# Small unused loads of a few rows each, put on three engines' queues between the large transfers of a cross-covariance attention kernel

## The chip, the cores and the metric

One core of one Trainium2 chip runs the kernel. The time is the device time of one execution in microseconds (us). The core has five engines that work side by side (PE multiplies matrices, DVE, ACT and POOL work on vectors, SP only issues transfers) and 16 DMA engines that move data between HBM and the on-chip memory. An engine runs its own instructions in order; engines wait for one another, and for transfers, through semaphores.

## The reference

Q, K and V are 8 x 12 x 512 x 64 in float32, as is the output: 12.58 MB each, 37.75 MB read and 12.58 MB written.

```
Q_norm = Q / (norm(Q, axis=-2) + 1e-10)          # over the 512 rows of a head
K_norm = K / (norm(K, axis=-2) + 1e-10)
attn   = softmax(einsum('bhnd,bhne->bhde', Q_norm, K_norm), axis=-1)   # 64 x 64 per head
out    = einsum('bhnd,bhde->bhne', V, attn)
```

## The kernel before

**Tiles.** The 96 heads are taken in S = 12 steps of 8 heads. A step loads one Q tile and one K tile (`load_qk`, L211-221, 128 partitions x 2 x 4 KB, 1 MB each), casts them to bfloat16 (`cast_qk`), squares them for the norms (`square`), forms the grams on PE (`grams`, L260), and goes through norms, softmax and scaling to `ab`. V comes in 12 tiles of 1 MB (`load_v`, L223-225, rows of 8 KB), is cast (`cast_v`), transposed on PE and multiplied with `ab` (`outs`, L338); `ocopy` brings the result to `so`, and `store` (L227-234) writes 1 MB per step. Step 0 loads its Q and K as halves of 512 KB, K's two from ACT's queue, all else from SP's. In all there are 52 transfers, 50 issued by SP and 2 by ACT.

**The cut store.** The store of step S - 3 (`PAR['SPLIT']`, `PAR['CUTS']`, L229-232) is written as three: 68 rows, 60 rows, and 128 rows of 4 KB.

**Order.** `Order` (L70 on) is a list scheduler that runs while the program is built: every piece of work is added with its cost, what it comes after and a rank; `plan.run()` fixes the order, and the loop at L484 emits the pieces in it. The order of the instructions on each engine is then fixed.

**Completion semaphores.** A transfer issued by SP or ACT takes, in the order of the program, the next of eight completion semaphores in turn (they are called slots below), and the built program makes its issue wait until the transfer eight places before it, which held the same slot, has landed. A semaphore counts to 16 for one transfer. As SP issues in order, all that stands behind a waiting issue waits too. At most eight of these transfers are thus in flight.

**Buffers.** Q and K share seven buffers (`NB['qk']`), V has three, `so` has six; a load also waits until the casts that read its buffer before are done.

Of the kernel before, what the change touches and what calls it, by code (L numbers as in the profile page):

```python
# [8 lines left out]
F32 = mybir.dt.float32  # L9
# [140 lines left out]
def kernel(  # L150
# [7 lines left out]
    nc = tc.nc  # L158
# [190 lines left out]
    def parts(s):  # L349
        return (0, 1) if s in FINE else (None,)  # L350

    for c in parts(0):
# [4 lines left out]
        name=nc.get_next_instruction_name(), engine=mybir.EngineType.Activation, ins=[], outs=[], act_func_set_id=LN_EXP))  # L357
# [29 lines left out]
    def v_at(v):  # L387
        return PAR["V_FROM"] + PAR["V_PACE"] * (v / W)
# [3 lines left out]
    def piece(key, engines, after, behind, rank, fn, *args):  # L392
        if key[0] in CHOICE:
            engines = {e: (c, BIAS.get((key[0], e), 0.0)) for e, c in engines.items()}
            plan.add(key, engines, after, behind, rank, lambda eng: fn(eng, *args))
        else:
            plan.add(key, engines, after, behind, rank, lambda eng: fn(*args))
# [46 lines left out]
    for w in range(W):  # L444
        for r in range(2):
            n = 2 * w + r - NB["v"]
# [22 lines left out]
    for s in range(S):  # L469
        for x in range(4):  # L470
            n = 4 * s + x - 2
# [7 lines left out]
        for i in halves(s):  # L479
            order = [("st", s, 0) if i else ("st", s - 1, halves(s - 1)[-1]) if s else None]  # L480
            piece(("st", s, i), {"DMA": 2 * X if i is None else X}, [("oc", s, x) for x in range(4)], order, v_at(0.5 * s) + PAR["ST_LAG"], store, s, i)

    ahead = [(k, 0, c) for c in parts(0) for k in ("lq", "lk")]
    for (emit, eng), (_, _, key, _) in zip(plan.run(), plan.order):  # L484
        if key not in ahead:
            emit(eng)


# [28 lines left out]
```

## Time and profile before

| | us |
|---|---|
| median of 2 runs (128.31 to 128.37) | 128.34 |
| the profiled execution, its own time | 128.12 |
| its span on the core | 126.0 |
| busy: PE 81.7, ACT 85.0, DVE 79.4, POOL 46.5 | |
| last instruction that computes ends | 114.8 |
| last store lands | 124.9 |

The page of the profile gives busy times by engine, a timeline in 40 slices, the DMA queues, and the chain of work that ended last. The timeline has lines for the DMA engines' busy share and for the GB/s moved. Queue q1 is that of SP's transfers, q10 that of ACT's, q8 fetches instructions. Beside the page, the trace keeps each DMA packet with its start, duration and size, and each count of a completion semaphore with its time; these are called packet records and counts below.

### The profile page before, as it was taken

To read this page: it belongs to the slowest core of one execution; us is meant where nothing else is said; L and a number is where in the kernel's file an instruction comes from. 1 tells how busy PE (TensorE), PEld (TensorE's weight loads), DVE (VectorE), ACT (ScalarE), POOL (GpSimd) and SP (SyncE) were. 2 spreads that over 40 slices of the span, in tenths; PEclk is the share of its full clock that TensorE was granted. 3 is DMA by queue.
4 is the path that set the end of the run, shared out by engine and by line. 5 is a ranking of instruction groups with operands and counts; after the bars stand their busy time and mean duration, and the time that the engine had idled before them with its cause. 6 is when DMAs were issued, how large, how long until landed. Compare 5 with 4: busy or idle time off the path is not lost.

```text
span 126.0 us, 4061 instructions
## 1 busy us (share of the span) xinstructions
PE 81.7 (65%) x1800; PEld 54.2 (43%) x1800; DVE 79.4 (63%) x140; ACT 85.0 (67%) x116; POOL 46.5 (37%) x40
## 2 busy tenths in 40 slices
PE   0009459894598787869578898864799878951000
PEld 0006145571474465557335556451387446630000
DVE  2223343899853989988987599993789998700000
ACT  4086668595697854998799987929839885864000
POOL 3250665470637098062707916144324700000000
PEclk9999999999657999995959999998559999996555
DMA  3999999999999999999999999999999999999982
GB/s 107 416 420 428 432 411 423 421 419 414 430 415 428 416 427 412 419 414 427 414 436 415 416 419 412 442 399 421 433 416 416 411 420 411 419 412 423 406 359 85
DMA packets 11588, 50.59 MB, mean 402 GB/s; under 512 B 819, under 2 KB 819, under 8 KB 10035
## 3 DMA queue, kind: packets, MB, share of 16 engines
q1 hardware_dynamic: 11283, 49.29, 95.3%
q10 hardware_dynamic: 288, 1.05, 2.0%
q8 instruction: 14, 0.23, 0.6%
q14 instruction: 3, 0.02, 0.0%
HBM read 37.75 MB, written 12.58 MB: 399 GB/s over the span
## 4 chain that ended last, share of the span: by engine, by line
DMA 54%; PE 15%; DVE 11%; ACT 6%; SPq 3%; issue 2%; ACTq 0%
DMA qk<-in_Q_dram 31%; DMA v<-in_V_dram 17%; DMA qk<-in_K_dram 6%; PE po L338 4%; ACT so L205 3%; PE l L266 3%; PE gram L260 3%; SPq L225 3%; DVE ab L310 2%; PE vps L323 2%; PE gram L289 2%; DVE s L271 1%; ACT sq L251 1%; DVE vt L207 1%; ACT vb L205 1%
## 5 line engine op out<-in xcount | busy, mean ns | idle before, releaser
L209 POOL TENSOR_SCALAR kb<-qk 128x2048 bf16<-128x2048 f32 (+1 forms) x13 | 23.4, 1802 | 38.1 <-DMA qk<-in_K_dram 35.0
L205 ACT COPY so<-po 128x512 f32<-128x512 f32 x47 | 25.6, 583 | 4.0 <-PE po L338 2.9
L251 ACT ACTIVATE sq<-qb 128x2048 bf16<-128x2048 bf16 (+1 forms) x13 | 23.1, 1778 | 7.7 <-DVE qb L207 7.6
L209 POOL TENSOR_SCALAR vb<-v 128x1024 bf16<-128x1024 f32 x15 | 20.1, 1355 | 13.7 <-DMA v<-in_V_dram 13.7
L338 PE MATMUL po<-ab,vt 128*32 128x128 bf16 x768 | 21.0, 237 | 6.0 <-ACT ex L299 1.6
L260 PE MATMUL gram<-qb,kb 32*128 32x128 bf16 x768 | 15.6, 240 | 12.2 <-POOL kb L209 9.6
L266 PE MATMUL l<-sq,hm 128*32 128x512 bf16 x96 | 19.5, 470 | 1.7 <-ACT sq L251 1.1
L323 PE MATMUL vps<-ident,vb 128*128 128x128 f32 x96 | 17.2, 305 | 4.4 <-POOL vb L209 2.3
L207 DVE CAST qb<-qk 128x2048 bf16<-128x2048 f32 (+1 forms) x12 | 13.6, 1135 | 10.0 <-DMA qk<-in_Q_dram 9.9
L260 PEld LDWEIGHTS <-kb 32*128 32x128 bf16 x768 | 13.4, 106 | 14.3 <-POOL kb L209 10.9
L338 PEld LDWEIGHTS <-vt 128*32 128x32 bf16 x768 | 14.3, 103 | 12.0 <-issue 7.7
L207 DVE COPY vt<-vps 128x1024 bf16<-128x1024 bf16 (+1 forms) x25 | 16.5, 664 | 3.0 <-PE vps L323 2.8
L251 ACT ACTIVATE sq<-kb 128x2048 bf16<-128x2048 bf16 (+1 forms) x10 | 17.3, 1734 | 0.7 <-POOL kb L209 0.7
L205 ACT CAST vb<-v 128x1024 bf16<-128x1024 f32 x9 | 12.1, 1344 | 6.8 <-DMA v<-in_V_dram 6.6
L323 PEld LDWEIGHTS vps<-ident,vb 128*128 128x128 f32 x96 | 11.3, 152 | 8.2 <-POOL vb L209 3.1
L271 DVE TENSOR_REDUCE s<-l 64x128 f32<-64x512 f32 x12 | 8.1, 678 | 8.5 <-PE l L266 8.5
L289 PE MATMUL gram<-ident,kqs 128*128 128x128 f32 x48 | 9.7, 336 | 3.5 <-DVE kqs L285 3.1
L295 DVE TENSOR_TENSOR ls<-gram,r 64x256 f32<-64x256 f32 x24 | 10.1, 420 | 2.7 <-PE gram L289 2.5
L285 DVE TENSOR_TENSOR kqs<-gram,r 128x512 f32<-128x512 f32 x12 | 8.2, 687 | 3.2 <-ACT r L281 2.6
L266 PEld LDWEIGHTS <-hm 128*32 128x32 bf16 x96 | 5.7, 108 | 9.7 <-issue 7.8
L310 DVE TENSOR_TENSOR ab<-ex,rb 128x512 bf16<-128x512 f32 x12 | 9.4, 781 | 0.4
L289 PEld LDWEIGHTS gram<-ident,kqs 128*128 128x128 f32 x48 | 6.2, 166 | 7.5 <-DVE kqs L285 6.6
(25 smaller groups left out, 41.3 us busy)
## 6 DMA issues: line engine op xcount, KB each, us to landing
v<-in_V_dram SPq DMA_DIRECT2D x12, 1024.0 KB, 19.5
qk<-in_Q_dram SPq DMA_DIRECT2D x11, 1024.0 KB, 19.6
qk<-in_K_dram SPq DMA_DIRECT2D x11, 1024.0 KB, 19.7
out_dram<-so SPq DMA_DIRECT2D x11, 1024.0 KB, 17.4
qk<-in_K_dram ACTq DMA_DIRECT2D x2, 512.0 KB, 6.0
qk<-in_Q_dram SPq DMA_DIRECT2D x2, 512.0 KB, 5.7
out_dram<-so SPq DMA_DIRECT2D x1, 512.0 KB, 10.0
out_dram<-so SPq DMA_DIRECT2D x1, 272.0 KB
```

The lines of the kernel that those rows point to most:

```text
L205: nc.scalar.copy(o, i)
L207: nc.vector.tensor_copy(o, i)
L209: nc.gpsimd.tensor_scalar(out=o, in0=i, scalar1=1.0, scalar2=0.0, op0=ALU.mult, op1=ALU.add)
L251: nc.scalar.activation(o, i, AF.Square)
L260: nc.tensor.matmul(gram[s][:, h, 0], k, q, start=(t == 0), stop=(t == TT - 1))
L266: nc.tensor.matmul(st[s][32 * x:32 * (x + 1)].rearrange("p t d -> p (t d)"), hm, sq[s][:, x, t:t + 4].rearrange("p t r d -> p (t r d)"), s ...
L271: nc.vector.tensor_reduce(out=s2[s], in_=st[s].rearrange("p t d -> p d t"), axis=mybir.AxisListType.X, op=ALU.add)
L289: nc.tensor.transpose(gram[s][:, h, 1], kqs[s][:, h], ident)
L295: nc.vector.tensor_tensor(out=ls[s][half], in0=gram[s][half, :, 1, half], in1=r12[s][half, :HU, None].to_broadcast([D, HU, D]), op=ALU.mult)
L310: nc.vector.tensor_tensor(out=ab[s], in0=ex[s][:, :, None, :].to_broadcast([128, HU, 2, D]), in1=rb[:, :, :, None].to_broadcast([128, HU, ...
L323: nc.tensor.transpose(ps[:, n], vb[w][:, j].rearrange("p r d c -> p (r d c)").bitcast(F32), ident)
L338: nc.tensor.matmul(po[s, x][32 * h:32 * (h + 1), j].rearrange("p r d -> p (r d)"), v, ab[s][:, h].rearrange("p r d -> p (r d)"), start=Tru ...
```

## The change

A function `mark` issues a load of n rows of K, of a few float32 words each, into a tile that nothing reads. After every planned transfer, from the seventh on, `marked` issues up to three of them: on SP's queue loads of 1, 2, ... 15 rows of 16 words, then one row of 18 words and 17 rows of 19 words; on ACT's queue eight loads of 1, 1, 2, 3, 5, 7, 17 and 20 rows of 20 to 34 words; on POOL's queue seven of 1, 1, 2, 3, 5, 17 and 24 rows of 42 to 54 words. The output does not depend on any of them.

```
+    marks = ctx.enter_context(tc.tile_pool(name="marks", bufs=1))
+    Km = K.rearrange("b h n d -> (b h n) d")
+    seen = [0]
+
+    shared = {q: (marks.tile([128, w], F32, name=f"marks{w}"), [0]) for q, w in ((nc.sync, 16), (nc.scalar, 36), (nc.gpsimd, 56))}
+
+    def mark(queue, n, words, at=0):
+        seen[0] += 1
+        if queue in shared and not (queue is nc.sync and words != 16):
+            m, next_row = shared[queue]
+            at = next_row[0]
+            next_row[0] += n
+        else:
+            m = marks.tile([128, words], F32, name=f"mark{seen[0]}")
+        queue.dma_start(out=m[at:at + n, 0:words], in_=Km[0:n, 0:words])
+
+    def marked(i):
+        if 1 <= i <= 15:
+            mark(nc.sync, i, 16)
+        for queue, gap, first, sizes in ((nc.scalar, 1, 3, (1, 1, 2, 3, 5, 7, 17, 20)), (nc.gpsimd, 2, 2, (1, 1, 2, 3, 5, 17, 24))):
+            k, rest = divmod(i - first, gap)
+            if rest == 0 and 0 <= k < len(sizes):
+                mark(queue, sizes[k], (20 if queue is nc.scalar else 42) + 2 * k)
+        if i == 16:
+            mark(nc.sync, 1, 18, 100)
+        if i == 17:
+            mark(nc.sync, 17, 19)
+
     ahead = [(k, 0, c) for c in parts(0) for k in ("lq", "lk")]
+    count = 0
     for (emit, eng), (_, _, key, _) in zip(plan.run(), plan.order):
         if key not in ahead:
             emit(eng)
+        if eng == "DMA":
+            count += 1
+            marked(count - 6)
```

The built program has 77 transfers on the eight slots in place of 52 (67 on SP, 10 on ACT), and 7 on POOL with semaphores of their own that only the end of the kernel waits for. The other instructions stand in the order they had. These are the first 33 of the 77, numbered in the order of the slots; a number n waits until n - 8 has landed. mS is a small load on SP with its rows, mA one on ACT; Q2 is the Q tile of step 2, V0 the first V tile.

```
 0 Q0a   1 K0a(ACT)  2 Q0b    3 K0b(ACT)  4 Q1     5 mA 1   6 K1    7 V0
 8 mA 1  9 mA 2     10 mA 3  11 mS 1     12 V1    13 mA 5  14 mA 7 15 mS 2
16 Q2   17 mA 17    18 mS 3  19 K2       20 mA 20 21 mS 4  22 V2   23 mS 5
24 Q3   25 mS 6     26 K3    27 mS 7     28 Q4    29 mS 8  30 K4   31 mS 9
32 V3
```

From 22 on, large loads and SP's small ones take turns up to number 47 (the load of 17 rows); from 48 on there are only large transfers.

## The prediction, written before the changed kernel was run

> **What bounds the kernel now.** I read the page's timeline first, then its queue table, then the busy times by stretch, then SP's own order of time.
>
> The page's timeline and queues:
>
> ```profile
> DMA  3999999999999999999999999999999999999982
> GB/s 107 416 420 428 432 411 423 421 419 414 430 415 428 416 427 412 419 414 427 414 436 415 416 419 412 442 399 421 433 416 416 411 420 411 419 412 423 406 359 85
> DMA packets 11588, 50.59 MB, mean 402 GB/s; under 512 B 819, under 2 KB 819, under 8 KB 10035
> ...
> q1 hardware_dynamic: 11283, 49.29, 95.3%
> q10 hardware_dynamic: 288, 1.05, 2.0%
> q8 instruction: 14, 0.23, 0.6%
> ```
>
> All 16 DMA engines are busy from the second slice to the last but one; no other engine is over 67%. The kernel is bound by its 50.3 MB, at about 421 GB/s, or 2.49 us for each 1 MB transfer. Busy times by stretch show the end:
>
> ```profile
> 110.00:115.00 5.00, 2.40 (x96) 1.46 (x88) 0.39 (x1) 3.51 (x7) 0.00 (x0) 0.94 1.02 413
> 115.00:120.00 5.00, 0.00 (x0) 0.00 (x0) 0.00 (x0) 0.00 (x0) 0.00 (x0) 0.50 1.02 413
> 120.00:123.00 3.00, 0.00 (x0) 0.00 (x0) 0.00 (x0) 0.00 (x0) 0.00 (x0) 0.50 0.85 350
> 123.00:126.00 3.00, 0.00 (x0) 0.00 (x0) 0.00 (x0) 0.00 (x0) 0.00 (x0) 0.50 0.18 72
> ```
>
> The five numbers before the last three are the engines' busy times, the last two the DMA share and GB/s. Computing ends at 114.8 us; the DMA engines need ten more. So computing can run some us late without moving the end, while every us that a DMA engine on the path loses is lost for good. From 120 us on the share falls: the 16 DMA engines do not end together. The counts of the last store show it: the 16 arrive from 121.06 to 124.91 us, three by 121.22, two more by 122.82, nine from 123.92 to 124.27, then 124.67 and 124.91. The span is set by the one engine that is last.
>
> SP's instructions in order of time, at the start:
>
> ```profile
> 5.42 0.38 SPq L219 DMA_DIRECT2D qk<-in_Q_dram  x1
> 5.84 0.47 SPq L219 DMA_DIRECT2D qk<-in_K_dram  x1
> 7.91 0.34 SPq L225 DMA_DIRECT2D v<-in_V_dram  x1
> 8.30 1.18 SPq L219 DMA_DIRECT2D qk<-in_Q_dram  x1
> 10.68 2.53 SPq L219 DMA_DIRECT2D qk<-in_K_dram  x1
> 13.31 3.12 SPq L219 DMA_DIRECT2D qk<-in_Q_dram  x1
> ```
>
> Start, duration, what. An issue takes 0.34 to 0.47 us; from 8 us on each lasts until there is room, since up to eight transfers are in flight (a Q load lands 19.6 us after its issue by the page, nearly 8 x 2.49). The queue is eight deep, far more than is needed to keep the engines fed.
>
> **The change part by part.** Nothing is removed. Added are 25 issues on the slots and 7 on POOL.
>
> *Issues on SP, 17.* At 0.33 us each (the cut stores' issues, the cheapest on SP, took 0.33 to 0.40) they are 5.6 us of SP, which has nothing to do but to keep the queue full. Cover: the transfers in flight. The small loads take slots, so fewer large ones are ahead. I walked through the list of slots with the landing times of before. Number 15 (mS 2) waits for 7 (V0, landed 15.5), and behind it on SP stands 16 (Q2). At that moment V1 alone is in flight, 2.49 us of work. Of it go 0.45 us (the 16 counts of one transfer are that far apart then), 0.33 us for the issue of mS 2, and about 1.0 us from the start of Q2's issue to its first packet (the first issue of the kernel: 0.74 to 1.75 us). 0.7 us are left: no gap, but a narrow place. Next K2 (19) goes out at about 16.8, V2 (22) at about 17.8; from Q3 on (waits for Q2, 20.5) three large transfers are in flight or more, 7.5 us of cover. Bounds for this place: 0 by these rows; 0.9 us lost if a small issue under load lasts as long as the median K issue, 1.93 us (1.93 - 0.33 - 0.7). I take 0, nearest to rows of like size. If the cover is gone, each us of delay is a us of time.
>
> *Issues on ACT, 8.* At 0.40 us (K's issues of before) 3.2 us, between 2.9 and 21 us, where ACT is idle 0.50, 1.23, 0.91, 0.31, 1.17 us between its instructions. Behind each stands ACT's next square or copy. Their waits are for transfers landed by then: the mA of 2 rows needs K0a (5.6) and comes after a square that ends 7.2; that of 20 rows needs V1 (18.0) and comes after one that ends at 20.2. Three gate SP in turn: mA 7 (14) gates V2, mA 17 gates mS 6, mA 20 gates Q4. mA 7 can go out when the square of Q1 ends, 13.8, and V2 has until about 22 us. ACT runs late by 1 to 2 us around 20 us; hidden by the ten us at the end. Cost 0.
>
> *Issues on POOL, 7.* The trace has no DMA issue on POOL. Between 0.33 us (SP's) and 1.9 us (POOL's longest instruction) each. POOL waits for data before the casts behind them: 3.84 (two of them), 1.31, 3.60, 1.17, 1.80, 3.91 us. At most 0.7 us late at one cast; hidden likewise. Cost 0.
>
> *Packets.* This is the cost that lands on the path. Rows: SP's 1 + ... + 15 + 1 + 17 = 138, ACT's 56, POOL's 76 (the two loads of one row go as 14 and 11 pieces), 270 small packets, and about 264 counts (4-byte packets; 122 from SP, 30 from ACT by the split below, 16 for each on POOL taken). How many DMA engines share them? The counts of before tell: the store of 68 rows got 12 of its 16 counts at its issue (109.6 us) and four at 117.10, 117.23, 117.76 and 117.82; that of 60 rows got one at once and 15 later; 128 rows all 16 late. So 4, 15 and 16 engines: the largest number up to 16 that divides the rows. A load of n rows up to 15 then lies on n engines, 17 rows on one, 20 on ten. I take the first engines to be used each time. Engine 0 then carries 15 + 1 + 17 rows from SP and 6 + 17 + 2 from ACT, 58, with some from POOL about 60, and 25 counts; engines 1 to 3 carry about 20, 18 and 16 rows and as many counts. The Trainium skill has the same in DMA: Bandwidth & Descriptors, "Why a DMA increments its semaphore by 16 and not by 1", and adds that the lowest-numbered engines are used on SP's and ACT's queues; the counts above agree with the numbers 4 and 15, and no run so far shows which engines they are. Spread evenly instead, 270 rows would be 17 an engine, and the sum below would be 0.4 us.
>
> The price of one row: the packet records have 9 ns for 4 bytes, 8 ns for 40 bytes, 156 to 159 ns for 4096 and 309 for 8192 bytes. A line through the last two is 9 ns + 0.037 ns a byte, 11 to 17 ns for 64 to 216 bytes. Ends: 9 and 159 ns. I take 20 ns, near the small rows, a little above the line since no packet of before reads so short a row from HBM. Engine 0: 60 x 20 + 25 x 9 = 1.4 us. Engines 1 to 3: 20 x 20 + 18 x 9 = 0.55 us. The same page, "Specifications", says that transfers under 512 bytes read, modify and write. That speaks for a dearer row; no record of before shows it, and it gives no figure.
>
> *What of it reaches the end.* The four engines of the 68 rows have 44 rows of 4 KB to go, 44 x 0.156 = 6.9 us: they end at 124.0, 124.1, 124.6 and 124.7. The last two counts, 124.67 and 124.91, are thus two of these four, and these four are the ones that get most of the small rows. If engine 0 is one of the late two: +1.4 us. If one of the early two (0.9 earlier): 1.4 - 0.9 = 0.5, and engines 1 to 3 give 0.55. The mean of 1.4 and 0.55 is 1.0 us.
>
> *Sum:* 128.12 + 0 + 0 + 0 + 1.0 = 129.1 for the profiled execution. The median of the runs shown is 0.22 above that execution, so 129.4.
>
> **The rivals.**
> - *Hidden.* The rows cost 9 ns, or engine 0 is an early one: 60 x 9 + 25 x 9 = 0.77, less than its 0.9 of room, and the others 0.3: about 128.5. For it: the 40-byte records. Against it: all four engines are close to the end. It needs no luck beyond a cheap row.
> - *The queue runs dry (slower).* At number 15 the wait for V0 leaves V1 alone in flight. If the small load's issue, or the wake-up, takes over 0.7 us more than I gave it, the DMA share shows a dip near 17 us. Price 0.9 us by the K issue row: 130.3; two such places, 131.2. For it: only one large transfer in flight, and an ACT queue whose late issue can hold SP. Against it: three in flight from 21 us on.
> - *Rows are dear (slower).* Engine 0 is then alone behind. From 47 ns a row the time is over 2% (47 x 60 + 0.2 - 0.45 = 2.57). At 60 ns: 3.4 us, 131.7; at the upper end of 159 ns 9.3 us, 137.7. For it: short reads that no record shows. Against it: the 40-byte and 4-byte records.
> - *Faster.* SP no longer stands in issues of 2 to 3 us, but a DMA share of 1.02 leaves nothing to gain. Only a lucky shift of the 14 instruction fetches (0.9 us each) to other engines could help.
>
> **How the numbers follow.** Likeliest, the rows on engine 0: 0.58, 129.4 (128.8 to 130.2). Hidden: 0.16, 128.5. Queue dry: 0.13, 130.3, a third of it over 2%. Rows dear: 0.11, 131.7 and more. Faster by any amount: 0.02. Two per cent, about what a measurement of this kernel can tell from no change, is 2.57 us, the bound 130.91. Slower: 0.11 + 0.04 = 0.15; faster 0.01; within 0.84. The range takes in the hidden case, the dry queue at two places, and the dear rows up to 60 ns: 128.3 to 131.7.
>
> **What would show it.** The DMA line stays at 9 in every slice up to 120 us, with no dip near 17; packets under 512 B rise from 819 by about 530; the last store's counts spread wider than 3.85 us, one engine alone at the end by up to 1.4 us; ACT's and POOL's busy times stay, computing ends within 2 us of 114.8. Wrong would be: a slice under 410 GB/s in the first 50 us (the dry queue); a last count over 2.5 us behind the others (dear rows); the last count unmoved (hidden).

## The result, and the profile after

The changed kernel takes 129.86 us (median of 2 runs, 129.84 to 129.87) against 128.34 before: 1.013 times as long, 95% interval 1.011 to 1.0151. The profiled execution took 129.84 us, with a span of 128.1 us against 126.0.

The page's timeline and queues of the changed kernel (of the queue lines: packets, MB, share of the 16 DMA engines):

```profile
DMA  3999999999999999999999999999999999999981
GB/s 115 402 416 425 432 339 391 402 350 416 413 428 414 424 426 407 416 414 434 406 425 432 411 418 417 432 407 422 424 425 415 412 417 415 422 409 415 412 368 45
DMA packets 12158, 50.62 MB, mean 395 GB/s; under 512 B 1389, under 2 KB 1389, under 8 KB 10605
...
q1 hardware_dynamic: 11543, 49.30, 94.8%
q10 hardware_dynamic: 374, 1.06, 2.2%
q8 instruction: 14, 0.23, 0.6%
q0 software_dynamic: 224, 0.01, 0.1%
```

The DMA engines are still at 9 everywhere, but the GB/s are not: slices 6 to 9 (16 to 29 us) show 339, 391, 402 and 350 where before they were 411 to 423. From slice 10 on the two kernels move the same. Busy times by stretch, first of the kernel before, then of the changed one (the last two columns are the DMA share and GB/s):

```profile
15.00:18.00 3.00, 1.11 (x4) 0.71 (x4) 1.53 (x3) 1.55 (x2) 1.35 (x2) 1.00 0.99 415
18.00:21.00 3.00, 2.86 (x69) 2.25 (x71) 1.51 (x4) 2.97 (x3) 1.62 (x2) 1.00 1.03 423
21.00:24.00 3.00, 2.60 (x28) 1.23 (x25) 1.44 (x3) 0.95 (x3) 1.62 (x1) 1.00 1.04 426
24.00:27.00 3.00, 2.86 (x74) 2.05 (x76) 2.73 (x5) 2.95 (x4) 2.10 (x2) 1.00 1.00 412
27.00:30.00 3.00, 2.48 (x61) 1.33 (x48) 2.93 (x3) 1.92 (x3) 1.15 (x1) 1.00 1.05 426
```

```profile
15.00:18.00 3.00, 1.11 (x4) 0.71 (x4) 1.25 (x3) 1.81 (x3) 2.12 (x3) 1.00 0.99 374
18.00:21.00 3.00, 2.57 (x68) 2.01 (x70) 1.74 (x5) 2.68 (x3) 1.33 (x1) 1.00 0.98 363
21.00:24.00 3.00, 2.60 (x32) 1.62 (x29) 1.67 (x3) 1.46 (x4) 1.03 (x1) 1.00 1.03 408
24.00:27.00 3.00, 1.96 (x27) 1.14 (x25) 2.57 (x5) 2.46 (x3) 2.91 (x3) 1.00 0.98 366
27.00:30.00 3.00, 2.58 (x90) 1.87 (x92) 1.23 (x1) 2.40 (x4) 2.53 (x3) 1.00 0.99 386
```

Two dips: 374 and 363 at 15 to 21 us, 366 and 386 at 24 to 30 us. I summed the bytes of the large packets that had ended by each moment, and divided the difference to before by 421 GB/s: the changed kernel is 0.1 to 0.2 us behind up to 17 us, 0.9 at 21, 1.0 at 24, 1.6 at 29, and then between 1.6 and 1.9 to the end. Nearly all the DMA time is lost in these two places.

SP's instructions in order of time show what stands there:

```profile
8.54 0.31 SPq L497 DMA_DIRECT2D marks<-in_K_dram  x1
10.85 0.35 SPq L225 DMA_DIRECT2D v<-in_V_dram  x1
15.79 0.25 SPq L497 DMA_DIRECT2D marks<-in_K_dram  x1
16.08 0.38 SPq L219 DMA_DIRECT2D qk<-in_Q_dram  x1
16.50 0.34 SPq L497 DMA_DIRECT2D marks<-in_K_dram  x1
16.89 0.38 SPq L219 DMA_DIRECT2D qk<-in_K_dram  x1
17.31 0.37 SPq L497 DMA_DIRECT2D marks<-in_K_dram  x1
17.72 0.52 SPq L225 DMA_DIRECT2D v<-in_V_dram  x1
18.29 0.35 SPq L497 DMA_DIRECT2D marks<-in_K_dram  x1
22.81 0.37 SPq L219 DMA_DIRECT2D qk<-in_Q_dram  x1
23.23 0.37 SPq L497 DMA_DIRECT2D marks<-in_K_dram  x1
23.71 0.37 SPq L219 DMA_DIRECT2D qk<-in_K_dram  x1
```

SP issues V1 at 10.85 and then stands until V0 has landed (its last count 15.77). Only then the 2-row load (L497) and Q2 (16.08) go out, when V1 alone is in flight. The first packet of Q2 starts at 17.25, 0.36 us before V1's first count (17.61). The DMA engines are hardly idle (in 15 to 18 us less than 0.1 us on the average of the 16), but of the 4 KB packets that start from then to 21 us, 32 take over 0.24 us in the packet records, and 19 of these 0.42 to 0.65, not 0.159. Q2's counts come from 20.47 to 22.80 (in the kernel before from 20.03 to 20.54); the last one lets Q3 go out, 2 us later than Q2 landed before. The second dip comes behind this; in it two packets that start at 25.2 us take 1.43 and 2.16 us. That Q3's late issue makes it is argued, not shown.

The end: the last store's counts come from 122.61 to 126.55 (before 121.04 to 124.89), the last 1.66 us later. No engine stands out: the last three are 126.19, 126.26 and 126.55. The rest of the span's 2.07 us, 0.41, lies behind the last count. 0.36 of it is one step on POOL in the final barrier (the instructions that end the kernel on all engines), from the trace's instructions (start in us):

```
before   125.327 GpSimd EVENT_SEMAPHORE (gather)   125.406 GpSimd EVENT_SEMAPHORE (release)
changed  126.904 GpSimd EVENT_SEMAPHORE (gather)   127.346 GpSimd EVENT_SEMAPHORE (release)
```

This step lengthens the span and not the time. The time grew by 1.72 us in this execution (128.12 to 129.84), the span by 2.07. In all 20 executions on record of the three kernels with POOL's seven loads the time is 1.73 to 1.82 us above the span; in those of the kernel before and of the kernels without a load on POOL it is 2.06 to 2.26. So the 1.66 us by which the last store lands late are nearly all that the time shows.

The small packets are cheap. Packet records of the changed kernel: 64 bytes 11 ns, 72 and 76 bytes 12 ns, 80 to 136 bytes 12 to 14 ns (two of 34), on POOL's queue 9 to 25 ns for 12 to 432 bytes.

### The profile page after: what moved, and what is told of

It reads as the page before. It is cut to its first block, busy times and chain, and to the rows that moved or that the text cites. A ratio compares the mean times of both kernels' runs of the same rounds, so it can differ in the third digit from the quotient of the medians.

```text
span 128.1 us, 4097 instructions
## 1 busy us (share of the span) xinstructions
PE 78.2 (61%) x1800; PEld 52.5 (41%) x1800; DVE 77.4 (60%) x140; ACT 85.7 (67%) x116; POOL 50.9 (40%) x47
## 4 chain that ended last, share of the span: by engine, by line
DMA 71%; PE 8%; ACT 4%; issue 2%; SPq 2%; DVE 2%; POOL 2%; ACTq 0%
DMA qk<-in_Q_dram 37%; DMA out_dram<-so 16%; DMA v<-in_V_dram 10%; DMA qk<-in_K_dram 7%; ACT so L205 4%; PE po L338 4%; PE vps L323 2%; POOL vb L209 2%; PE gram L289 2%; SPq L219 1%; DVE kqs L285 1%; DVE qb L207 1%; SPq L221 1%; SPq L497 0%; PE l L275 0%
## 5 line engine op out<-in xcount | busy, mean ns | idle before, releaser
L209 POOL TENSOR_SCALAR vb<-v 128x1024 bf16<-128x1024 f32 x15 | 20.8, 1402 | 12.6 <-DMA v<-in_V_dram 8.5
L207 DVE CAST qb<-qk 128x2048 bf16<-128x2048 f32 (+1 forms) x12 | 13.6, 1137 | 11.2 <-DMA qk<-in_Q_dram 11.1
L266 PE MATMUL l<-sq,hm 128*32 128x512 bf16 x96 | 18.2, 450 | 2.3 <-ACT sq L251 2.2
L323 PE MATMUL vps<-ident,vb 128*128 128x128 f32 x96 | 16.3, 292 | 3.3 <-DVE vt L207 1.8
L323 PEld LDWEIGHTS vps<-ident,vb 128*128 128x128 f32 x96 | 10.4, 144 | 7.1 <-DVE vt L207 2.9
L289 PE MATMUL gram<-ident,kqs 128*128 128x128 f32 x48 | 8.9, 316 | 4.2 <-DVE kqs L285 3.9
```

The source lines that it names most:

```text
L207: nc.vector.tensor_copy(o, i)
L209: nc.gpsimd.tensor_scalar(out=o, in0=i, scalar1=1.0, scalar2=0.0, op0=ALU.mult, op1=ALU.add)
L266: nc.tensor.matmul(st[s][32 * x:32 * (x + 1)].rearrange("p t d -> p (t d)"), hm, sq[s][:, x, t:t + 4].rearrange("p t r d -> p (t r d)"), s ...
L289: nc.tensor.transpose(gram[s][:, h, 1], kqs[s][:, h], ident)
L323: nc.tensor.transpose(ps[:, n], vb[w][:, j].rearrange("p r d c -> p (r d c)").bitcast(F32), ident)
```

## The experiments

Three theories. **Slots:** the small loads hold so many of the eight slots that too few bytes are in flight, and the queue runs short at the two places. **Rows:** the first DMA engines carry more small rows and end late (the likeliest case of the prediction). **POOL's transfers:** they slow the others, two of them being issued at 17.1 and 24.8 us. All kernels leave the computation as it is; each is told by its edit to the changed kernel.

### Each queue's loads by themselves

SP's 17 loads alone:

```
-        for queue, gap, first, sizes in ((nc.scalar, 1, 3, ...), (nc.gpsimd, 2, 2, ...)):
+        for queue, gap, first, sizes in ():
```

> Only SP's 17 small loads, none on ACT or POOL. Slots (the queue runs short where ACT's and SP's small loads together hold seven of the eight slots and V1 alone is in flight): with SP's alone every second slot is a large transfer, V1, Q2 and K2 are in flight when V0 lands, so 128.4 to 128.7 and no slice under 405 GB/s before 50 us. Rows (the first DMA engines carry more small rows): 33 of engine 0's 60 rows, at 12 ns 0.4 us, with its counts 0.55: 128.9. POOL's transfers: as before, 128.3.

ACT's 8 alone (the lines that issue SP's are out, and the loop has ACT's entry only):

> Only ACT's 8 small loads. Slots: V1 goes out at 8.3 us, Q2, K2 and V2 right behind it, so three or more large transfers stay in flight: 128.3 to 128.6, no dip. Rows: 25 rows on engine 0, 0.3 us, with counts 0.4: 128.7. POOL's transfers: 128.3. If ACT's issues themselves cost (ACT runs late), over 128.8.

POOL's 7 alone:

> Only POOL's 7 small loads, which take none of the eight slots. Slots: no dip in GB/s; the time is that of before plus the longer end on POOL (0.36 us in the changed kernel between the last two steps of the final barrier), 128.3 to 128.7. Rows: nearly none, 128.4. POOL's transfers (they slow the others at 17 and 25 us, where two of them are issued): the dips at 15 to 21 and 24 to 30 us are there, 129.3 or more.

SP's and ACT's without POOL's:

> SP's and ACT's small loads, without POOL's. Slots: the order of the slots is that of the changed kernel, so both dips in GB/s (15 to 21 and 24 to 30 us) stay and the time is 129.4 to 129.9. Rows: 58 rows on engine 0, about 1 us, but additive: the sum of what SP alone and ACT alone cost. POOL's transfers: 128.5 or less, no dips.

| loads | us | ratio to before, 95% interval | span |
|---|---|---|---|
| SP's | 128.15 | 0.9999 (0.9987 to 1.001) | 125.9 |
| ACT's | 128.34 | 1.0004 (0.9981 to 1.0026) | 125.9 |
| POOL's | 128.63 | 1.0042 (1.002 to 1.0064) | 126.6 |
| SP's and ACT's | 129.72 | 1.0115 (1.0086 to 1.0143) | 127.7 |

SP's cost nothing (less than the 128.4 expected), ACT's cost nothing, together they cost 1.15%. Rows by themselves can't do that: if SP's 33 on one DMA engine fit the 0.9 us of room that the prediction gives it, all 58 take 1.6 us at most, 0.7 more than the room. GB/s of SP's alone, ACT's alone, and both:

```profile
GB/s 102 418 422 437 423 413 421 417 422 414 421 426 417 419 427 409 417 412 432 409 432 417 418 419 415 434 406 422 422 432 414 409 419 411 415 414 415 424 367 98
```

```profile
GB/s 108 415 419 423 433 415 415 420 422 416 419 427 428 412 428 411 415 416 428 411 433 424 410 420 414 431 412 419 429 424 414 411 423 411 414 411 427 410 355 95
```

```profile
GB/s 105 408 425 427 423 338 402 416 404 421 413 429 416 420 426 406 418 415 426 412 434 418 416 422 417 427 410 422 428 417 416 410 419 410 423 407 422 399 332 46
```

Slices 6 to 9 are 413, 421, 417, 422 and 415, 415, 420, 422 by themselves, and 338, 402, 416, 404 together. POOL's loads alone have no dip. The same step of the final barrier takes 0.44 us, but it is not in the time, as shown above. The profiled execution (128.33 us, last count 124.99) is 0.1 to 0.2 us behind by 10 us and stays so; a kernel below without a load on POOL is 0.2 behind there too. Its other executions go up to 129.27 us, one of 131.07 aside; where these lose time no trace shows, so the rest of the ratio's 0.4% is not explained.

In the profiled execution of SP's and ACT's loads (129.87 us) the bytes that had ended are 1.1 us behind from 60 us on, yet the last count comes 1.8 us late (126.72). The rest arises at the end, where the DMA engines finish further apart than before; why they do is open.

### The same loads, one behind each large transfer

```
-        queue.dma_start(out=m[at:at + n, 0:words], in_=Km[0:n, 0:words])
+        nc.sync.dma_start(out=m[at:at + n, 0:words], in_=Km[0:n, 0:words])
...
+        if 18 <= i <= 25:
+            k = i - 18
+            mark(nc.scalar, (1, 1, 2, 3, 5, 7, 17, 20)[k], 20 + 2 * k)
```

> The 25 small loads of SP and ACT, with the same rows and words, all on SP's queue, one behind each large transfer from the seventh on; none on POOL. Slots: three or four large transfers in flight all the time, so no dip: 128.0 to 128.4, as with SP's 17 alone, against 129.7 with ACT's on ACT's queue. Rows: engine 0 still carries 58 rows and 25 counts: 128.8 to 129.4, as if the queue did not matter.

128.12 us, ratio 0.9977 (0.9953 to 1.0001), last count at 124.88. Its GB/s:

```profile
GB/s 104 415 427 428 424 419 416 419 424 411 418 423 430 410 427 412 419 410 429 407 433 417 418 418 414 437 402 420 424 428 418 409 420 411 416 414 418 415 363 105
```

The same 25 loads with the same rows cost nothing once they stand one behind each large transfer. The rows, then, are hidden at this size, and what costs is where the loads stand.

### The first place alone, and the kernel without it

Of SP's loads only the first two, with ACT's eight:

```
-        if 1 <= i <= 15:
+        if 1 <= i <= 2:
```

> ACT's eight loads and of SP's only the first two (1 and 2 rows of 16 words); none on POOL. The slots up to number 15 are those of the changed kernel, so V1 alone is in flight when V0 lands. Slots: the dip at 15 to 21 us stays, the second one at 24 to 30 us goes, as Q3 need not wait for Q2: 128.8 to 129.2. Rows: 28 rows on engine 0, 128.6 at most, with no dip.

The changed kernel with all loads but these two, POOL's too:

```
-        if 1 <= i <= 15:
+        if 3 <= i <= 15:
```

> The changed kernel less SP's first two small loads (of 1 and 2 rows); all the others stay, POOL's too. Slots: V1 goes out at 8.3 and Q2 at 8.8 us, so two large transfers or more are in flight from there on; the two dips at 15 to 30 us go. What is left is the longer end on POOL, as with POOL alone: 128.4 to 128.8. Rows: engine 0 has 56 of its 58 rows: 129.5 or more, as changed.

With the two: 129.69 us, ratio 1.0086 (1.0053 to 1.012). Without the two: 128.69 us, ratio 1.0042 (1.0012 to 1.0073), the same as with POOL's loads alone. Stretches of the kernel with the two only:

```profile
15.00:18.00 3.00, 1.11 (x4) 0.71 (x4) 1.53 (x3) 1.52 (x3) 1.34 (x2) 1.00 1.01 356
18.00:21.00 3.00, 2.94 (x70) 2.27 (x72) 1.51 (x4) 3.00 (x3) 1.33 (x1) 1.00 0.95 351
21.00:24.00 3.00, 2.54 (x31) 1.44 (x27) 1.98 (x4) 1.46 (x4) 1.69 (x1) 1.00 1.05 424
24.00:27.00 3.00, 1.65 (x24) 1.07 (x24) 2.20 (x4) 2.38 (x2) 1.33 (x2) 1.00 0.99 407
27.00:30.00 3.00, 2.16 (x80) 1.97 (x80) 1.23 (x1) 1.62 (x2) 2.52 (x2) 0.62 1.03 423
```

The first dip is there (356, 351) and the second is all but gone (407, 423); by the bytes that had ended, 1.0 us is lost at 21 us and 1.0 to 1.1 from there on. Without the two loads SP goes on early, and the GB/s hold:

```profile
GB/s 111 388 417 430 425 417 421 417 413 425 420 412 436 405 426 417 412 420 421 418 427 424 406 422 418 432 406 423 426 421 412 415 413 413 421 413 419 412 330 41
```

Two loads of three rows of 64 bytes in all make the dip, because of the slots that they take. The median with the two, 129.69, is higher than expected (128.8 to 129.2); the ratio of 1.0086 is what 1.1 us would give. Its 10 runs go from 128.55 to 130.15 us, and the profiled one is the slowest of them. Its last count, 127.06, is 2.2 us later than before and 1.05 us behind the other fifteen. So the dip explains half of what this execution lost; the other half lies with one DMA engine at the end, and no run shows why it is late (its small rows and counts, 28 and 10 at most, are 0.4 us).

### How much must be in flight

Three and two loads of one row behind each of fifteen large transfers, on SP, none else:

```
         if 1 <= i <= 15:
-            mark(nc.sync, i, 16)
+            for _ in range(3):      # range(2) in the other kernel
+                mark(nc.sync, 1, 16)
```

> Three loads of one row of 16 words behind each of fifteen large transfers, on SP; none on ACT or POOL. Two of eight slots hold large transfers. Slots: when one lands, one is left in flight, 2.5 us, for an issue of four (1.3 us) and the way to the first packet (1.0 us and more): the narrow place of the changed kernel fifteen times. If each costs 0.3 to 0.8 us as there, 132 to 140 us and GB/s under 400 from 8 to 50 us. Rows: 45 rows of 12 ns on engine 0, 0.5 us, with 45 counts: 129.2 at most.

> Two loads of one row of 16 words behind each of fifteen large transfers, on SP; none else. Each time a large transfer lands that SP waits for, two large ones are left in flight, 5 us, where three small loads each left one. Slots: 5 us cover the issues (1.0 us) and the way to the first packet: 128.0 to 128.6, no dip. If two are still too few, half of what three cost or more: 131 and up.

Three: 134.05 us in the fastest of four executions, which is the profiled one, against 128.26 for the kernel before; the others took 136.68 to 138.81. Two: 128.74 us, ratio 1.0037 (1.0006 to 1.0067), runs from 127.87 to 129.64. GB/s of three, then of two:

```profile
GB/s 115 412 421 432 430 308 354 332 301 304 404 400 400 276 414 438 384 422 410 426 410 437 414 416 420 420 426 411 420 430 416 411 415 416 411 419 416 415 366 68
```

```profile
GB/s 127 408 419 429 435 410 429 409 417 414 409 406 423 410 386 348 382 410 433 413 423 431 405 422 417 429 411 418 428 423 413 413 415 415 424 405 423 410 366 69
```

With one large transfer left in flight at each issue, slices 6 to 17 fall as low as 276, and the profiled execution is 5.7 us behind at 60 us: 0.4 us for each of the fifteen places. With two left there is nothing up to 30 us, but a dip of 386, 348 and 382 at 44 to 54 us that cost 1.3 us in this execution and nothing in the fastest. So 5 us of work in flight is the edge, not the safe side as I had expected; what made the dip there was not tried.

### What a row on one DMA engine is worth

```
-        if 1 <= i <= 15:
-            mark(nc.sync, i, 16)
+        if 24 <= i <= 27:
+            mark(nc.sync, 113, 18)
```

> Four loads of 113 rows of 18 words on SP between the 30th and 34th transfer, none else. 113 has no divisor up to 16 but 1, so 452 rows lie on one DMA engine. It measures what a row is worth at the end. At the 12 ns of the packet records 5.4 us on one engine; less up to 0.9 us of room if it is one of the early of the four: 132.6 to 133.8, with one count of the last store 4 us or more behind the other fifteen. If short rows overlap with the long ones of the same engine and cost nothing, 128.3. If they are dearer than their record, over 134.

133.28 us, ratio 1.0362 (1.0301 to 1.0423): in the expected range, and not for the expected reason. The last store's counts end at 128.69, 128.85, 128.94 and 130.32, so no engine is 4 us behind the others; all had lost some 4 us by 100 us. The 452 rows did run on one engine, 113 at a time, 8.2 ns from start to start. SP's instructions show the rest:

```profile
56.66 0.71 SPq L497 DMA_DIRECT2D mark<-in_K_dram  x1
59.25 11.77 SPq L219 DMA_DIRECT2D qk<-in_K_dram  x1
71.06 1.45 SPq L497 DMA_DIRECT2D mark<-in_K_dram  x1
72.61 2.75 SPq L219 DMA_DIRECT2D qk<-in_Q_dram  x1
```

The K issue behind the first load of 113 rows lasts from 59.25 to 71.02 us. It is not a wait, though the view of waits puts 11.1 us of it down to a copy on DVE, the last that ended before: its slot was free at 59.2, and DVE's count had been at 52 since 58.52, with which two other kernels of this document had this issue done. The first 113 rows themselves ran only from 72.29 to 73.21 us. So the issue stood while one engine had 113 small rows waiting behind its large ones, and ended some 1.3 us before they ran. What held the issue, no run shows. This run, then, doesn't tell what a row is worth at the end. Loads of 17 rows do (15 of them, to a tile of their own; the columns are set so that no two overlap):

```
-        if 1 <= i <= 15:
-            mark(nc.sync, i, 16)
+        if 1 <= i <= 15:
+            mark(nc.sync, 17, 18)
```

> One load of 17 rows of 18 words behind each of fifteen large transfers, on SP; none else. [...] In the run with 113 rows they followed each other at 8.2 ns; 255 of them are 2.1 us, with 12 ns 3.1 us. Rows (time on one engine reaches the end once it is past that engine's 0.9 us of room): 129.3 to 130.5, with one count of the last store late by 1 us or more against before. Slots: three large transfers in flight as with SP alone, so by themselves 128.1.

129.53 us, ratio 1.0099 (1.0083 to 1.0115), and no dip from 15 us on. The counts of the last store, in us:

```
before    ... 124.17 124.24 124.25 124.65 124.89
rows_17   ... 124.31 124.34 124.64 124.77 126.30
```

One engine alone is late, 1.41 us after the end of before. Its 255 rows at 8.2 ns and 15 counts at 9 ns are 2.2 us, so without them it would have ended at about 124.1, with 0.8 us of room. That fits one of the two early engines of the four; which engine it is, the records don't say.

### One load on POOL

```
-        ... ((nc.scalar, 1, 3, ...), (nc.gpsimd, 2, 2, (1, 1, 2, 3, 5, 17, 24))):
+        ... ((nc.gpsimd, 2, 2, (1,)),):
```

(SP's lines are out too.)

> One load of one row on POOL's queue, none else. If the longer final barrier on POOL comes with the use of its queue at all, its step takes 0.36 us more as with seven loads, and the time is 128.4 to 128.7, the same as with seven. If it comes with the number of loads, 128.1 to 128.3.

128.41 us, ratio 1.0014 (0.9989 to 1.0038). The step of the final barrier takes 0.083 us, as before (0.079); with seven loads it takes 0.44. It does not come with the use of POOL's queue as such; whether it is the number of loads, their rows or their semaphores stays open. The expectation took the step for a part of the time, and that failed: with the short step the time is 128.41, in the range that was given for the long one. Here the time is 2.24 to 2.32 us above the span, 0.16 more than without a load on POOL, and nothing in the trace shows where that lies.

## Why the prediction was right, and where it was wrong

The time, 129.86, lies near the 129.4 that was forecast. The way to it was another: of the two terms that decide, one was put at 1.0 us and is nothing, the other at nothing and is about 1.65 us. That the sums are so near to each other is luck. Of the prediction's own signs, the one for the dry queue came true (slices of 339, 391, 402 and 350 GB/s; a 407 near 50 us stands in the kernel before too), and the one for its likeliest case, one engine alone at the end, did not.

- **The bound.** Right: the 16 DMA engines, at 421 GB/s, with room for the computing. ACT's and POOL's busy times hardly moved (85.7 and 50.9 us, the second with seven issues of 0.53 to 0.69 us).
- **Issues on SP, "I take 0".** This step failed. The place was the right one (number 15, V1 alone in flight) and the loss of some 0.8 us by 21 us lies within the bound of 0.9, but not for its reason: the bound took a small issue of 1.93 us, and it took 0.25. Nor is there the dip of the DMA share that the rival named: the share is 0.99 and 0.98, the GB/s fall. The 0.7 us of room that I worked out were 0.36: V0's last count came 0.27 us later than before, and the first packet 1.17 us after the issue, not 1.0. And I took it that room of any size costs nothing. It doesn't hold: Q2's packets had begun before V1's ended, yet some took up to four times their length for some us. Why a queue that is refilled so late restarts slowly, no run shows.
- **The second place** I did not see: I let Q3 go out at 20.5, when Q2 lands. Q2's 16 counts are 2.3 us apart, not 0.45, and the slot is free only with the last. (In the kernel before, too, they are 1.6 us apart or more from the next transfer on, so the 0.45 held for the first ones alone.) With SP's first two and ACT's loads alone this cost some 0.1 us more, with all of SP's and ACT's 0.2, with POOL's too 0.7. What POOL's loads add there is not settled.
- **Issues on ACT, cost 0.** Right for ACT's own time: the ratio is 1.0004, and an issue (0.23 to 0.29 us, the first one 0.50) mostly runs while ACT's instruction before it still computes. But their price was their slots, and there I looked for a late issue (mA 7, mA 17, mA 20), not for their number.
- **Issues on POOL, cost 0.** Right as far as the runs tell: without POOL's loads the time is 129.72, with them 129.86. Their 0.36 us in the final barrier are in the span and not in the time. By themselves they come to a ratio of 1.0042 (1.002 to 1.0064), which is not explained.
- **Packets.** Packets rose by 570, not 530, as POOL's queue has 224 and not 188. On SP's and ACT's queues the count was right: 122 more 4-byte packets on q1, 30 on q10, and one engine for 17 rows. The rule of the Trainium skill (DMA: Bandwidth & Descriptors, "Why a DMA increments its semaphore by 16 and not by 1") thus agrees; the counts of the run with 17 rows fit one of the four engines that the 68-row store uses. The price was mis-sized: 20 ns taken, 11 to 14 ns in the records, 8 to 10 ns from start to start, as the line through 4 and 8 KB had it. The same page's read, modify and write under 512 bytes ("Specifications") shows in no price here: 64-byte rows take 11 ns. With 58 rows at 10 ns and 25 counts at 9 ns engine 0 has 0.8 us more, just its room. So the rival "hidden" was right on the rows, and the rival "the queue runs dry" on the rest.
- **Chances.** The dry queue got 0.13, too little: the room of 0.7 us was a difference of rows with errors of that size, and the upper bound of 0.9 us at that place was as near as 0.

## What to carry to other kernels

What kept this DMA-bound kernel fed is bytes in flight, and a scheme that counts transfers (here eight completion semaphores in turn) lets a load of 64 bytes hold as much of it as one of 1 MB. Before small transfers are added to such a queue, walk through its slots and ask at each issue how many us of large transfers are left in flight: three or more of these transfers (7.5 us) cost nothing here, two were the edge, one cost about 0.4 us at each of fifteen places and 0.8 to 1.0 us at a single one. A busy share of 9 in every slice does not show it; GB/s does.

## What the runs showed of the hardware that was not expected

- Small rows on one DMA engine follow each other at 8.2 ns (72 bytes); that is about a twentieth of the 159 ns of a 4 KB row.
- Behind a load of 113 rows, all on one engine, the next issue on the same queue lasted 11.8 us, with its slot free and DVE's count there. Loads of 17 rows were issued in 0.29 to 2.28 us each.
- POOL's load of 17 rows of 208 bytes was not put on one engine, as SP's and ACT's were: its records are eight packets of 416 bytes, two rows each, and one of 212, which start from 28.67 to 30.34 us and not one behind the other.
- Seven loads issued by POOL lengthen one step of the final barrier from 0.08 to 0.44 us, and the time outside the span is 0.35 us shorter with them.
- Small loads on ACT's queue started late under load: of 7 rows 3.4 us after the issue (13.37 to 16.75 us), of 17 rows 2.2 us (15.30 to 17.55), where Q2 on SP's queue took 1.17.
